# RWKV stage of a hybrid trunk: a strictly ordered opening with fill products in it, two directions filled before their evictions, 44 products kept for the end

## The chip, the cores and the metric

The kernel runs on one core of a Trainium2 chip. The metric is the device time of one execution in microseconds. All arithmetic is in fp32 (the large projections in a high and a low fp32r part).

## What is computed

One inference step of a trunk of two layers with 128 context tokens and 1024 latent tokens of width 1024. In each layer the normed and modulated input is projected to four branches (mLSTM, RG-LRU, retention, RWKV-7), each in both directions of time; their outputs, times a SiLU gate, go together through one output projection to the residual. The change is in the RWKV branch:

```python
def rwkv_scan(r, w, k, v, kk, bb, s0):
    def step(s, xs):
        rt, wt, kt, vt, kkt, bt = xs
        sa = jnp.einsum('bhij,bhj->bhi', s, -kkt)
        s = s * wt[:, :, None, :] + sa[..., None] * bt[:, :, None, :] + vt[..., None] * kt[:, :, None, :]
        return s, jnp.einsum('bhij,bhj->bhi', s, rt)

def rwkv_branch(u, mu, w0, w2, a0, a2, k_k, k_a, r_k, s0, rows):
    ...
    for d in range(N_DIR):
        w_log = -jax.nn.softplus(-(w0[d] + lw @ w2[d])) - 0.5
        decay = jnp.exp(-jnp.exp(w_log))
        a = jax.nn.sigmoid(a0[d] + la @ a2[d])
        kt = k * (1.0 + (a - 1.0) * k_a)
        seqs = (r, decay, kt, v, kk, kk * a)
        ...
        y, sf = rwkv_scan(*seqs, s0[:, d])
    bonus = jnp.sum(r * k * r_k, -1, keepdims=True) * v
    y = (head_norm(outs[0] + outs[1]) + bonus) * jax.nn.silu(g)

# of the layer
u = h @ p['w_in']
y = jnp.concatenate([y_a, y_b, y_c, y_d], -1) @ p['w_out']
x = x + gate * y
```

## The kernel before

A layer has three parts: the input projection, with the mLSTM, RG-LRU and retention branches laid over it; the RWKV stage (`rw_all`, from L160); and `tail` (L1171), which multiplies the last part of the output projection, adds the residual and norms for the next layer.

**Units.** The RWKV stage works the sequence in chunks of 64. Nine units follow one another: two halves of the chunks for each of four pairs of heads, and one unit for the context tokens at index 6. Forward and backward direction ("f", "b") of a unit run side by side. The steps of a unit are: the block of its pair (`rw_block`: token shift, norm, sums over heads); `early` (`rw_prep`: the lora products `a<-lora_x`, decay scans, the operands AR and BK); `scores` (products `a<-AR,BK`, masked into SC); `solve` (L494: the inverse of 32x32 triangular blocks; the blocks go by DMA from SC through DRAM into the tiles iU and iN, iN is cleared by two memsets on GpSimd, 62 operations on VectorE, DMAs back into SC); `tokens` (transposes); `mid` (L526: five steps of products that put the blocks together, evicted into NT, Wt, SC, AR, UV); and the chain (`rw_chain`, L577: sixteen gaps in which state ST and UV follow from each other in tiles `u`, then the output `u` evicted into y). `rw_final` norms y and stores it.

**Fills.** Between these steps TensorE gets "fill" products, L1289, `main<-yt,ow`, and modulation products, `main<-wmod`, from one generator: the input projection of the RWKV pairs 1 to 3 (96 products each), in layer 0 also the next layer's modulation, and the output projection of what is finished. `pull(x)` takes x of them, `drain(q)` takes all up to a mark. The output projection loads an old value through the tile xi, adds to it and stores it, and once four units' worth is finished it covers the RWKV pairs 0 to 2 too. Their weights (`ow`, 6 buffers) and inputs (`yt`, 16 buffers) come by DMA; all DMAs are issued from one queue, SP.

**Order.** A scheduler orders instructions on each engine by a priority (`level` 0 to 3, 3 first) and by what it reckons to be ready. While `self.strict` is true, each product that goes through `pm`, `ptr` or `fill` is chained to the one before, so TensorE follows the program. The opening of the stage (all up to `mid` of unit 0, with the preparation of unit 1) is not strict and runs at level 1; the units are strict. In a unit `pull(rate)` is called in each gap, with rate = what is left / units left / 20. PSUM tiles: `a` (two buffers), `v` and `u` (two banks each, one buffer), `main`.

Of the kernel before, what the change touches and what calls it, by code (L numbers as in the profile page):

```python
# [16 lines left out]
MUL, ADD, SUB, MAX, MIN = ALU.mult, ALU.add, ALU.subtract, ALU.max, ALU.min  # L17
# [13 lines left out]
class B:  # L31
# [130 lines left out]
    def rw_all(self, l):  # L162
# [5 lines left out]
        N = len(units)  # L168
# [3 lines left out]

        def block(n):
            p = units[n][0]
            if n < N and p not in P:
                for q in LATE:
                    if p is None or q == p:
                        self.drain(q)
                with self.level(1):
                    P[p] = self.rw_block(l, p)  # L180

        def early(n):
            p, su = units[n]
            S[n] = {}
            for dn in "fb":
                with self.level(1):
                    S[n][dn] = self.rw_prep(P[p], dn, 0 if p is None else 8 * su if dn == "f" else 8 - 8 * su, self.rd[n % 2])
                yield

        def operands(n, lv):  # L190
            with self.level(lv):
                for dn in "fb":
                    self.rw_operands(P[units[n][0]], dn, S[n][dn])
# [32 lines left out]

        run = lambda g: [None for _ in g]
        self.strict = False
        block(0)
        run(early(0))  # L230
        operands(0, 1)
        run(scores(0, 1))
        solve(0)
        run(tokens(0))
        run(early(1))
        operands(1, 1)
        run(scores(1, 1))
        self.drain(1)
        run(mid(0))
        self.last, self.strict = None, True  # L240
        total = self.nfill
        left = lambda: total - self.pulled
        finish = None
        for n, (p, su) in enumerate(units):
            if n + 1 < N:
                solve(n + 1)
            rate = left() / (N - n) / (16 + (4 if n + 1 < N else 0))
            steps = self.rw_chain(l, P[p], su, S[n], S[n - 1] if su else None)
            tok = tokens(n + 1) if n + 1 < N else iter(())
            pre = iter(())  # L250
            for gap in range(16):
# [17 lines left out]
                if gap in (12, 14):  # L269
                    next(pre, None)  # L270
            run(tok)
            run(pre)
            with self.level(3):
# [5 lines left out]
            for k in range(5):  # L279
                next(m, None)  # L280
                self.pull(rate * 0.8)
                if k >= 2:
                    next(sc, None)
            run(m)
            run(sc)
            if su or p is None:
                finish = P[p]
        with self.level(1):
            self.rw_final(l, finish)
# [11 lines left out]
    def drain(self, what):  # L301
        while what not in self.done:
            next(self.fills)

# [189 lines left out]
    def rw_solve(self, S):  # L494
# [15 lines left out]
        self.a.copy(U[b], N[b][:, ::-1])  # L510
        self.g.memset(N, 0.0)
        self.g.memset(N[:, ::33], -1.0)  # L512
        Uv, Nv = U.rearrange("p (r k) -> p r k", k=32), N.rearrange("p (r k) -> p r k", k=32)
# [12 lines left out]
    def rw_mid(self, S):  # L526
# [30 lines left out]
        for d, dn in enumerate("fb"):  # L557
            AR, SC, UV = (S[dn][n] for n in ("AR", "SC", "UV"))
            for g in range(4):
                for h in range(2):  # L560
                    for q in range(2):
                        self.pm(ps[HV[h], q, d, g], UV[HV[q], 2 * g + q, HV[h]], SC[HV[q], 4 * q + g, h, 0:64])
            self.a.copy(AR[:, 0::2, 0], ps[:, 0, d])
            self.v.tensor_copy(AR[:, 1::2, 0], ps[:, 1, d])
        yield
        ps = self.pst2("u").rearrange("p d (g h x) -> p d g h x", h=2, x=64)
        for d, dn in enumerate("fb"):
            SC, UV = S[dn]["SC"], S[dn]["UV"]
            for g in range(4):
                for h in range(2):  # L570
                    for q in range(2):
                        self.pm(ps[HV[q], d, g, h], SC[HV[q], 4 * q + g, h, 0:64], SC[HV[q], 4 - 4 * q + g, h, 0:64])
            uv = lambda q: UV[HV[q], q::2].rearrange("p g (h i) -> p g h i", h=2)
            self.a.copy(uv(0), ps[HV[0], d])
            self.v.tensor_copy(uv(1), ps[HV[1], d])

    def rw_chain(self, l, X, su, S, prev):  # L577
# [13 lines left out]
        for i in range(8):  # L591
# [21 lines left out]
            yield  # L613
        po = self.pst2("u")
        for di, dn in enumerate("fb"):
            s = S[dn]
            if p is None:
                for q in range(4):
                    self.dma(self.o["rwkv_s"][l, di, q], s["ST"][:, 4 + q])
            ps = po[:, di].rearrange("p (c i) -> p c i", i=64)  # L620

            first = True
            for j, a, _ in D[dn]:
                if a is not None:
                    for h in HV:
                        self.pm(ps[h, j], a[h], s["AR"][h, j, 1], start=first, stop=False)
                    first = False
            for i, (j, a, _) in enumerate(D[dn]):
                for h in range(2):
                    self.pm(ps[HV[h], j], s["UV"][:, j, HV[h]], s["SC"][:, 4 * (j % 2) + j // 2, h, 64:128], start=False, stop=(i == 7))  # L630
            y = X["y"][:, 64 * s["c0"]:64 * s["c0"] + 512].rearrange("p (c i) -> p c i", i=64)
            if su or (p is None and di):
                self.tt(self.v, y, ps, y, ADD)
            else:
                self.a.copy(y, ps)

# [808 lines left out]
MLB = 1  # L1445
YOB = 16
HV = (slice(0, 64), slice(64, 128))

# [154 lines left out]
```

## Time and profile before

| | us |
|---|---|
| median of three runs | 4093.64 |
| lowest, highest | 4092.91, 4098.87 |
| the profiled execution | 4099.86 |
| its span, first to last instruction | 4098.1 |
| TensorE busy in the span | 3655.4 (89%) |
| VectorE, ScalarE, GpSimd busy | 2001.2, 1295.3, 1135.2 |

The mean granted clock of TensorE was 0.923 of its full speed. The RWKV stage lies, by the first and last of its products, between about 1102 and 2059 us in the first layer and between 3151 and 4051 us in the second; the rest of the span is input projection, tail and start. In what follows "opening" is from the first lora product to the first chain product, "body" the units 0 to 7, "end" from the last unit's last chain product to the tail's first product. TensorE appears in the trace with two records for one fp32 product. A wait in square brackets is the idle time of the engine just before the row, with what ended it.

### The profile page before, as it was taken

The page shows a single profiled execution, that of the slowest core. Times are in us where ns is not written, and L with a number is a line of the kernel's source. Part 1 is how long each engine was busy: PE and PEld are TensorE (multiplying, and loading weights), DVE is VectorE, ACT ScalarE, POOL GpSimd, SP SyncE. Part 2 cuts the span into 40 slices and gives each one's busy share as a digit, 9 for nine tenths or more (in the row PEclk, how much of TensorE's full clock was granted, in tenths as well). Part 3 has the DMA queues.
Part 4 walks back from the last instruction along what each step waited for, and adds up shares of the span by engine and source line. Part 5 has one row for each costly group of instructions (what it writes and reads, how often), then busy time and mean ns, then how long its engine had stood idle before and what let it go on. Part 6 is the DMA issues. An engine that isn't in the chain of part 4 may idle for free. (4 is left out here: it accounts for less than half of the span.)

```text
span 4098.1 us, 69587 instructions
## 1 busy us (share of the span) xinstructions
PE 3655.4 (89%) x28050; PEld 2844.9 (69%) x28050; DVE 2001.2 (49%) x3917; ACT 1295.3 (32%) x2102; POOL 1135.2 (28%) x1052
## 2 busy tenths in 40 slices
PE   6899999999959898989779999999998598988896
PEld 3889899999544455555468898999985455555554
DVE  4454643333264565565274545533331746656544
ACT  3244422122223333332152535122122234333312
POOL 4223234533221112212043232434431212212200
PEclk8999999999969999999989999999998699989998
DMA  5434443443624543444644434543445144433445
GB/s 210 120 120 138 122 133 121 121 132 123 214 62 146 158 137 119 120 122 116 191 157 132 122 115 129 139 127 94 136 137 180 29 130 131 131 113 101 117 141 166
DMA packets 413550, 538.02 MB, mean 131 GB/s; under 512 B 141708, under 2 KB 322700, under 8 KB 413228
## 3 DMA queue, kind: packets, MB, share of 16 engines
q1 hardware_dynamic: 413228, 533.57, 42.8%
q8 instruction: 221, 3.62, 0.4%
q14 instruction: 101, 0.83, 0.1%
HBM read 387.17 MB, written 146.25 MB: 130 GB/s over the span
## 5 line engine op out<-in xcount | busy, mean ns | idle before, releaser
L1289 PE MATMUL main<-yt,ow 128*128 128x384 f32 x2592 | 963.9, 512 | 18.0 <-DVE xi L48 12.0
L1289 PEld LDWEIGHTS main<-yt,ow 128*128 128x128 f32 x2592 | 473.9, 194 | 314.2 <-issue 37.2
L59 PE MATMUL main<-hh,wring_h 128*128 128x384 f32 x1824 | 648.5, 356 | 26.8 <-DVE st L1283 15.5
L59 PE MATMUL main<-hl,wring_h 128*128 128x384 f32 x1824 | 645.4, 354 | 13.7 <-DVE hl L44 10.9
L59 PE MATMUL main<-hh,wring_l 128*128 128x384 f32 x1824 | 641.4, 352 | 0.0
L44 POOL TENSOR_TENSOR wring_l<-raw,wring_h 128x1024 fp32r<-128x1024 f32 x100 | 243.8, 2442 | 592.2 <-ACT wring_h L1240 444.5
L59 PEld LDWEIGHTS main<-hh,wring_h 128*128 128x128 f32 x1824 | 359.7, 197 | 40.1 <-DVE st L1283 16.2
L59 PEld LDWEIGHTS main<-hl,wring_h 128*128 128x128 f32 x1824 | 359.6, 197 | 25.6 <-DVE hl L44 13.5
L59 PEld LDWEIGHTS main<-hh,wring_l 128*128 128x128 f32 x1824 | 359.6, 197 | 7.6 <-issue 1.3
L59 PE MATMUL main<-wring_h,hh 128*128 128x256 f32 x864 | 261.3, 302 | 14.0 <-DVE st L1283 13.0
L59 PE MATMUL main<-wring_l,hh 128*128 128x256 f32 x864 | 257.2, 298 | 0.0
L59 PE MATMUL main<-wring_h,hl 128*128 128x256 f32 x864 | 256.5, 297 | 0.0
L44 DVE TENSOR_TENSOR tm<-iU,iN 64x31 f32<-64x31 f32 (+15 forms) x558 | 191.9, 344 | 92.8 <-POOL iN L512 77.9
L44 POOL TENSOR_TENSOR t<-s_k,bb 128x512 f32<-128x512 f32 x36 | 60.4, 1678 | 576.3 <-ACT bb L56 576.3
L1283 DVE COPY st<-main 128x384 f32<-128x384 f32 (+1 forms) x168 | 86.1, 512 | 258.1 <-PE main L59 227.0
L44 DVE TENSOR_TENSOR iN<-iN,tm 64x31 f32<-64x31 f32 (+15 forms) x558 | 198.0, 355 | 16.5
L59 PEld LDWEIGHTS main<-wring_h,hh 128*128 128x128 f32 x864 | 173.9, 201 | 19.6 <-DVE st L1283 14.0
L59 PE MATMUL a<-AR,BK 64*128 64x128 f32 x1152 | 125.4, 324 | 58.3 <-POOL BK L44 30.4
L59 PEld LDWEIGHTS main<-wring_h,hl 128*128 128x128 f32 x864 | 173.9, 201 | 4.6 <-issue 0.4
L59 PEld LDWEIGHTS main<-wring_l,hh 128*128 128x128 f32 x864 | 173.6, 201 | 3.0
L59 PEld LDWEIGHTS a<-AR,BK 64*128 64x128 f32 x1152 | 108.4, 222 | 96.1 <-POOL BK L44 34.9
L1240 ACT CAST wring_h<-raw 128x1024 fp32r<-128x1024 f32 x100 | 103.4, 1046 | 219.8 <-PE main L59 169.4
(332 smaller groups left out, 6110.4 us busy)
## 6 DMA issues: line engine op xcount, KB each, us to landing
raw<-in_w_in SPq DMA_DIRECT2D x100, 512.0 KB
ow<-in_w_in SPq DMA_DIRECT2D x144, 256.0 KB
ow<-in_w_out SPq DMA_DIRECT2D x144, 256.0 KB
yt<-h SPq DMA_DIRECT2D x144, 192.0 KB
mrb<-mlrow SPq DMA_DIRECT2D x48, 384.0 KB
x<-xi SPq DMA_DIRECT2D x96, 192.0 KB
yt<-y SPq DMA_DIRECT2D x90, 192.0 KB
wmod<-in_w_mod SPq DMA_DIRECT2D x64, 256.0 KB
```

The costliest lines, as they stand in the source:

```text
L44: return e.tensor_tensor(out=out, in0=a, in1=b, op=op)
L59: return self.t.matmul(out, l, r, start=start, stop=stop)
L1240: self.a.copy(hi, raw)
L1283: self.v.tensor_copy(q[:, :w], ps[:, :w])
L1289: return self.pe(self.t.matmul(*a, **k))
```

## The change

First, the opening is strict too, at levels 2 and 3 for unit 0, and after each of its steps fill products are taken (`weave(g, x)`: x after each step of g). Second, the rate in the units leaves 44 products (`RESERVE`), which are taken at the end: 11 ahead of `rw_final` of the last unit, 33 behind it; this `rw_final` has level 3 instead of 1. Third, in the last two steps of `mid` and in the chain's output both directions' products come first and all evictions behind them. Fourth, the two memsets of the solve move from GpSimd to VectorE. The number of instructions of each kind stays as it is.

```diff
-        def block(n):
+        def block(n, lv=1):
...
-                with self.level(1):
+                with self.level(lv):
                     P[p] = self.rw_block(l, p)
...
-        def early(n):
+        def early(n, lv=1):
...
-        run = lambda g: [None for _ in g]
-        self.strict = False
-        block(0)
-        run(early(0))
-        operands(0, 1)
-        run(scores(0, 1))
+        def weave(g, x):
+            for _ in g:
+                self.pull(x)
+
+        self.last, self.strict = None, True
+        block(0, 2)
+        weave(early(0, 3), 8)
+        operands(0, 3)
+        weave(scores(0, 3), 3)
         solve(0)
-        run(tokens(0))
-        run(early(1))
+        weave(tokens(0), 3)
+        weave(early(1, 1), 4)
         operands(1, 1)
-        run(scores(1, 1))
+        weave(scores(1, 1), 4)
         self.drain(1)
-        run(mid(0))
-        self.last, self.strict = None, True
+        weave(mid(0), 2)
...
-            rate = left() / (N - n) / (16 + (4 if n + 1 < N else 0))
+            rate = (left() - RESERVE) / (N - n) / (16 + (4 if n + 1 < N else 0))
...
-        with self.level(1):
+        self.pull(RESERVE / 4)
+        with self.level(3):
             self.rw_final(l, finish)
         self.finished += 1
         self.drain("all")
...
-        self.g.memset(N, 0.0)
-        self.g.memset(N[:, ::33], -1.0)
+        v.memset(N, 0.0)
+        v.memset(N[:, ::33], -1.0)
...
         for d, dn in enumerate("fb"):
-            AR, SC, UV = (S[dn][n] for n in ("AR", "SC", "UV"))
+            SC, UV = S[dn]["SC"], S[dn]["UV"]
...
+        for d, dn in enumerate("fb"):
+            AR = S[dn]["AR"]
             self.a.copy(AR[:, 0::2, 0], ps[:, 0, d])
             self.v.tensor_copy(AR[:, 1::2, 0], ps[:, 1, d])
...
+        for d, dn in enumerate("fb"):
+            UV = S[dn]["UV"]
             uv = lambda q: UV[HV[q], q::2].rearrange("p g (h i) -> p g h i", h=2)
             self.a.copy(uv(0), ps[HV[0], d])
             self.v.tensor_copy(uv(1), ps[HV[1], d])
...
-            y = X["y"][:, 64 * s["c0"]:64 * s["c0"] + 512].rearrange("p (c i) -> p c i", i=64)
+        for di, dn in enumerate("fb"):
+            y = X["y"][:, 64 * S[dn]["c0"]:64 * S[dn]["c0"] + 512].rearrange("p (c i) -> p c i", i=64)
             if su or (p is None and di):
-                self.tt(self.v, y, ps, y, ADD)
+                self.tt(self.v, y, po[:, di], y, ADD)
             else:
-                self.a.copy(y, ps)
+                self.a.copy(y, po[:, di])
...
+RESERVE = 44
```

**TensorE, second layer, from the end of retention into the opening.** `ntr` are the transposes of retention's norm, `sq` and `rk` feed sums over heads. Before:

```order
L1289 MATMUL main<-yt,ow 128x384 x20
L682 MATMUL ntr<-ident,rty 128x128 x4
L1289 MATMUL main<-yt,ow 128x384 x11
L682 MATMUL ntr<-ident,rty 128x128 x4
L1289 MATMUL main<-yt,ow 128x384 x9
L682 MATMUL ntr<-ident,rty 128x128
L1289 MATMUL main<-yt,ow 128x384 x8
L59 MATMUL a<-lora_x,lora_w 128x512 x2
L59 MATMUL v<-sq,bones 128x512
L1289 MATMUL main<-yt,ow 128x384
L59 MATMUL a<-lora_x,lora_w 128x512 x2
```

And now:

```order
L689 MATMUL ntr<-ident,rty 128x128 x9
L59 MATMUL a<-lora_x,lora_w 128x512 x2
L59 MATMUL v<-sq,bones 128x512
L1296 MATMUL main<-yt,ow 128x384 x8
L59 MATMUL a<-lora_x,lora_w 128x512 x2
L59 MATMUL v<-sq,bones 128x512
L1296 MATMUL main<-yt,ow 128x384 x8
L59 MATMUL v<-rk,bones 128x512 x2
L59 MATMUL a<-AR,BK 128x128 x8
L1296 MATMUL main<-yt,ow 128x384 x3
L59 MATMUL a<-AR,BK 128x128 x8
```

The fill products moved from between retention's last steps to between the opening's.

**VectorE, first layer, inside the first solve.** `tm` and `iN` are the solve's operations, the others the preparation of unit 1 and the masks of its scores. Before:

```order
L44 TENSOR_TENSOR tm<-iU,iN 64x207
L52 TENSOR_SCALAR tw<-tw 128x512
L44 TENSOR_TENSOR iN<-iN,tm 64x23x9
L400 SCALAR_TENSOR_TENSOR bb<-scan_87,tw 128x512
L44 TENSOR_TENSOR tm<-iU,iN 64x220
L44 TENSOR_TENSOR iN<-iN,tm 64x22x10
L52 TENSOR_SCALAR tw<-tw 128x512
L44 TENSOR_TENSOR tm<-iU,iN 64x231
L44 TENSOR_TENSOR AR<-kk,tw 128x8x63
```

And now:

```order
L44 TENSOR_TENSOR tm<-iU,iN 64x207
L44 TENSOR_TENSOR iN<-iN,tm 64x23x9
L44 TENSOR_TENSOR tm<-iU,iN 64x220
L44 TENSOR_TENSOR iN<-iN,tm 64x22x10
L44 TENSOR_TENSOR tm<-iU,iN 64x231
L44 TENSOR_TENSOR iN<-iN,tm 64x21x11
L44 TENSOR_TENSOR tm<-iU,iN 64x240
L44 TENSOR_TENSOR iN<-iN,tm 64x20x12
```

The other work stands behind 46 of the 62 operations instead of behind 17.

**TensorE, second layer, behind the last unit's chain.** `yq` feeds the head sums of `rw_final`, `t_yh` and `t_hi` are the tail's operands. Before:

```order
L59 MATMUL u<-AR,ST 64x64 x16
L59 MATMUL u<-SC,UV 64x64 x16
L59 MATMUL v<-yq,bones 128x512 x2
L59 MATMUL main<-t_yh_33021,t_hi 128x384 x4
L59 MATMUL main<-t_yl_33022,t_hi 128x384
```

And now:

```order
L59 MATMUL u<-AR,ST 64x64 x16
L59 MATMUL u<-SC,UV 64x64 x16
L1296 MATMUL main<-yt,ow 128x384 x5
L59 MATMUL v<-yq,bones 128x512
L1296 MATMUL main<-yt,ow 128x384 x6
L59 MATMUL v<-yq,bones 128x512
L1296 MATMUL main<-yt,ow 128x384 x33
L59 MATMUL main<-t_yh_33021,t_hi 128x384
```

All 44 kept products stand ahead of the tail here; in the first layer the last 18 stand among the tail's products, in groups of three.

## Rows read from the trace of the kernel before

**Rows 1.** Stretches: length; busy of PE, PEld, DVE, ACT, POOL; PEclk, DMA share, GB/s.

```profile
1101.90:1223.70 121.80, 79.19 (x665) 54.55 (x664) 72.02 (x151) 38.59 (x68) 40.31 (x29) 0.71 0.31 93
1223.70:1966.10 742.40, 663.56 (x7061) 397.24 (x7061) 415.01 (x986) 246.24 (x452) 141.60 (x116) 0.95 0.44 129
1966.10:2033.10 67.00, 58.96 (x383) 32.13 (x382) 23.12 (x63) 0.63 (x1) 0.00 (x0) 0.97 0.61 180
2033.10:2059.30 26.20, 3.20 (x4) 0.80 (x4) 6.55 (x8) 9.16 (x10) 7.13 (x3) 0.59 0.91 315
...
3150.80:3265.40 114.60, 59.92 (x585) 45.08 (x584) 72.38 (x151) 36.18 (x63) 40.40 (x29) 0.59 0.18 51
3265.40:3969.50 704.10, 625.19 (x6952) 392.91 (x6952) 414.42 (x984) 242.77 (x446) 141.73 (x116) 0.95 0.41 120
3969.50:4033.80 64.30, 54.83 (x371) 30.04 (x370) 21.43 (x58) 0.63 (x1) 0.00 (x0) 0.98 0.62 184
4033.80:4051.30 17.50, 4.15 (x4) 1.00 (x4) 4.39 (x7) 6.14 (x7) 0.00 (x0) 0.50 0.87 293
```

**Rows 2.** Timeline of PE, second layer, end of retention: start, length, instruction, count.

```profile
3118.74 13.12 PE L1289 MATMUL main<-yt,ow 128*128 128x384 f32 x40
...
3132.13 7.26 PE L1289 MATMUL main<-yt,ow 128*128 128x384 f32 x22
...
3150.84 1.13 PE L59 MATMUL a<-lora_x,lora_w 64*128 64x512 f32 x4
```

**Rows 3.** Timeline of POOL, first and second layer, end of retention.

```profile
1044.76 0.45 POOL L44 TENSOR_TENSOR rtR<-rtR,rtU 64x128 f32<-64x128 f32 x1
...
3074.58 0.45 POOL L44 TENSOR_TENSOR rtR<-rtR,rtU 64x128 f32<-64x128 f32 x1
3125.12 3.19 POOL L44 TENSOR_TENSOR rty<-rty,nss 128x1152 f32<-128x1152 f32 x1 [50.10 <-ACT nss L56]
```

**Rows 4.** Timeline of PE, second layer, opening; idle before a row in brackets.

```profile
3241.15 0.59 PE L59 MATMUL v<-ident,SC 32*32 32x32 f32 x4 [12.96 <-DMA SC<-dN]
```

**Rows 5.** Timeline of DVE, first layer: the first solve's first and last operation.

```profile
1150.96 0.20 DVE L44 TENSOR_TENSOR tm<-iU,iN 64x31 f32<-64x31 f32 x1 [7.64 <-POOL iN L512]
...
1195.43 0.18 DVE L44 TENSOR_TENSOR iN<-iN,tm 64x31 f32<-64x31 f32 x1
```

**Rows 6.** Page, part 5: one of the solve's two operations: busy, mean ns, idle.

```profile
L44 DVE TENSOR_TENSOR tm<-iU,iN 64x31 f32<-64x31 f32 (+15 forms) x558 | 191.9, 344 | 92.8 <-POOL iN L512 77.9
```

**Rows 7.** Waits of PE in both bodies, layer by layer: us in total, times, longest.

```profile
PE u L59 <- DVE y L44: 18.6, 3, 6.5
...
PE v L59 <- DVE AR L564: 8.3, 8, 1.1
PE u L59 <- DVE UV L575: 8.1, 8, 3.5
PE u L59 <- ACT y L635: 6.1, 5, 1.9
...
PE main L1289 <- DMA wmod<-in_w_mod: 1.0, 3, 0.6
...
PE u L59 <- DVE y L44: 20.3, 3, 7.0
...
PE u L59 <- ACT y L635: 8.4, 5, 2.6
PE v L59 <- DVE AR L564: 7.5, 7, 1.1
```

**Rows 8.** SP and PE timelines in one unit: the solve's way back, first use.

```profile
1464.31 4.44 SPq L81 DMA_DIRECT2D SC<-dN  x8
...
1486.49 0.75 PE L59 MATMUL v<-ident,SC 32*32 32x32 f32 x64
```

**Rows 9.** Timelines of PE and SP at the end of the second layer's stage.

```profile
4051.35 1.65 PE L59 MATMUL main<-t_yh,t_hi 128*128 128x384 f32 x4 [11.22 <-ACT t_yh L1202]
...
4030.31 13.16 SPq L81 DMA_DIRECT2D xs<-x  x24
```

More of the change, by code (lines that the diff above doesn't have):

```diff
@@ L185, in early @@
             for dn in "fb":
-                with self.level(1):
+                with self.level(lv):
                     S[n][dn] = self.rw_prep(P[p], dn, 0 if p is None else 8 * su if dn == "f" else 8 - 8 * su, self.rd[n % 2])
@@ L270, in rw_all @@
                     next(pre, None)
-            run(tok)
-            run(pre)
+            weave(tok, 0)
+            weave(pre, 0)
             with self.level(3):
@@ L283, in rw_all @@
                     next(sc, None)
-            run(m)
-            run(sc)
+            weave(m, 0)
+            weave(sc, 0)
             if su or p is None:
                 finish = P[p]
-        with self.level(1):
+        self.pull(RESERVE / 4)
+        with self.level(3):
             self.rw_final(l, finish)
@@ L302, in drain @@
         while what not in self.done:
-            next(self.fills)
+            next(self.fills, None)
     def rw_block(self, l, p):
@@ L613, in rw_chain @@
             yield
-        po = self.pst2("u")
+        po = self.pst2("u").rearrange("p d (c i) -> p d c i", i=64)
         for di, dn in enumerate("fb"):
-            s = S[dn]
+            s, ps = S[dn], po[:, di]
             if p is None:
@@ L619, in rw_chain @@
                     self.dma(self.o["rwkv_s"][l, di, q], s["ST"][:, 4 + q])
-            ps = po[:, di].rearrange("p (c i) -> p c i", i=64)
             first = True
```

## The prediction

> **What bounds the kernel now.** I read the table of stretches first. In the bodies of the two RWKV stages TensorE is busy 663.56 of 742.4 us and 625.19 of 704.1 us [rows 1], so there time falls only if TensorE gets less to do or waits less. The reader should see next how different the openings are: 79.19 of 121.8 us busy at a granted clock of 0.71, and 59.92 of 114.6 us at 0.59 [rows 1]. They run a chain of small steps and waits, and the fill products that could cover them have been used up: in program order 56 output products and 16 modulation products (layer 0), 95 (layer 1) stand before the first lora product. The timeline of the end of retention shows those products in wide blocks, 40 records of them 13.12 us long between a retention product and the norm's transposes [rows 2]. A product is two records. A block of 22 took 7.26 us, so the 18 more of the other cost 13.12 - 7.26 = 5.86 us, 0.65 us a product [rows 2]. The waits of the bodies come third: they are led by waits of one direction's products for the other direction's eviction [rows 7]. Last, the ends of the stages: 26.2 and 17.5 us with TensorE busy 3.20 and 4.15 us, but DMA at 0.91 and 0.87 of its share, 315 and 293 GB/s [rows 1].
>
> The sum is made against the profiled execution's own 4099.86 us (span 4098.1). The median of the three runs is 4093.64, so 6 us come off at the end.
>
> **The opening.** The fills leave the end of retention, which then runs on its own latencies. GpSimd's retention recurrence ends at 1044.8 (layer 0) and 3074.6 (layer 1) [rows 3], 57 and 76 us ahead of the first lora product. What remains is some ten score and state products with a mask each, and then a norm: in layer 1 it took from 3118.74, where the last retention product was done, to 3128.31 [rows 2, 3], 9.6 us; transposes and their evictions follow. I allow 28 us from the end of the recurrence: first lora product at 1073 and 3103, where they were at 1101.9 and 3150.84 [rows 1, 2].
>
> From there TensorE has more work than before. Its own part: the layer 1 opening, with only one fill product in it, was busy 59.92 us at clock 0.59 [rows 1]; at full clock that is 59.92 x 0.59 = 35 us. Fill in program order: 96 output products and 25 modulation products in layer 0, 105 output products in layer 1. At 0.65 us, and 0.87 for a modulation product (an estimate: 512 columns instead of 384), this is 62 + 22 = 84 us and 68 us. To this I add 5 us of waits and 4 us of low clock at the start, since TensorE idles at the end of retention: 1073 + 35 + 84 + 9 = 1201 and 3103 + 35 + 68 + 9 = 3215 for the first chain product, against 1223.7 and 3265.4. That is **-23 and -50**.
>
> The other path to the same point is the latency path, and it must be shorter for this to hold. Before, the first solve took from 1150.96 to 1195.6 [rows 5], because operations of the second unit's preparation were put between its own 62; these are some 0.35 us each [rows 6], 22 us, and with gaps about 26. In the new order 46 of them stand in a row, so the matrices are back some 18 us earlier, and the 12.96 us wait for them [rows 4] goes. The whole path from lora to chain was 121.8 and 114.6 us [rows 1]; less 18 and less the 13, it is some 90. It lies below the 112 to 128 of TensorE, so TensorE sets the end, if the DMAs of the solve are not held up; that is a rival below.
>
> In strict order a fill product that waits for its weights holds every product behind it. The bodies have run so all along, and there the wait for weights was 1.0 us in all, in 3 times [rows 7]; I take zero, and for the upper bound the loss of the whole gain, 73 us. The Trainium skill, TensorE: Matmul & The Clock Gate, section Part 3: Packing small matmuls, says that matmuls are strictly first in, first out and are never reordered. By that rule nothing passes a fill that waits, the row does not contradict it, and the sum would lie between the -73 taken here and 0 for this term.
>
> **Fewer fills in the bodies.** Units 0 to 7 hold 447 output and 39 modulation products instead of 485 and 47 in layer 0, and 444 instead of 490 in layer 1. At the same prices: 38 x 0.65 + 8 x 0.87 = **-32**, 46 x 0.65 = **-30**. This is on the path, because TensorE is busy nine tenths there [rows 1]. Unit 8 has 61 instead of 68 and 55 instead of 61: -4.5 and -4, and with the y wait between its directions **-7 and -6**.
>
> **Both directions first, then the evictions.** The waits for y fall away: 18.6 and 6.1 us in layer 0, 20.3 and 8.4 in layer 1 [rows 7]. The evictions that ended late (up to 7.0 us, DVE being in the middle of a solve) are next needed when the same banks are filled again, four steps of the next unit's middle later. The waits of the middle for AR and UV, 8.3 and 8.1 us, of which 3.5 is in the opening, and 7.5 in layer 1 [rows 7], go only in half: the next step now finds two pairs of evictions outstanding instead of one, with two fill products over them. So 24.7 + 6.4 = **-31**, 28.7 + 3.8 = **-32**.
>
> **The end.** 44 products, 28.6 us at 0.65, now stand behind the last unit. Before the tail's first product TensorE waited 11.22 us [rows 9], which covers as much; that leaves 17 in layer 1, where 33 of the 44 stand before the tail. In layer 0, 18 stand among the tail's own products, so less: 5 at the least. By DMA it is more. Unit 8 moved 180 GB/s over 67 us for 68 products [rows 1], 0.18 MB for each, so 44 bring 7.8 MB to a stretch that was already at 293 to 315 GB/s: 25 to 27 us. I take **+16 and +22**, nearer to the DMA rows in layer 1, since that stretch was full.
>
> **The memsets on DVE.** No row shows one there. The solve's operations of at most 256 elements take 0.18 to 0.4 us [rows 5, 6]; 1024 elements should be 0.2 to 1.4 us, nine times a layer. DVE gets 1 us later to what is queued behind, and waited for GpSimd's memset 77.9 us in all [rows 6], which may shrink. Bounds -10 to +15 a layer; taken **+5 each**, mostly for evictions behind a solve.
>
> **Sum:** -23 -50 -32 -30 -7 -6 -31 -32 +16 +22 +5 +5 = -163. 4099.9 - 163 = 3937, less 6 for the median: **3931**, told as 3930.
>
> **Rivals.**
> (a) The opening's gain is not had. In the new order the solve's small DMAs stand on SP's queue between loads of weights whose buffers come free only when fill products have run; TensorE, in strict order, then waits in the middle for the inverse, as it did for 12.96 us [rows 4]. Against it: 25 output products in layer 1 stand between the last score and the middle as cover. If all is lost: 3930 + 73 = 4003; I put it at **3995**.
> (b) The end jams. If the 44 products run at unit 8's rate, 67 us / 68 = 0.985 us [rows 1], they take 43 us, less 11 covered: 32; and if the tail's loads also stand behind the 13.16 us of residual loads on SP [rows 9], some 45 a layer instead of 19: 3930 + 52 = **3982**.
> (c) The fused evictions only move the wait: the refill of the same banks waits for y instead. Then the 63 us stay: **3993**. Against it are the four steps between.
> (d) The clock gains too: bodies at 0.95 [rows 1] go to 1.0 once fewer waits break them. 5% of 1289 busy us is 64; about three quarters of it: **3880**.
> (e) Slower: the solve becomes the bound of every unit. Its matrices were on the way at 1464.31 to 1468.75 and first used at 1486.49 [rows 8], 17.7 us of slack. Units become some 7 us shorter and the memset takes 1, so about 10 are left. If DVE's new order (a solve with its evictions behind two directions) delays it by more than those 10, each further us costs 16 of them (eight solves in each layer that a body waits for). From 20.2 us of delay on all of the 163 is lost; at 21.2 the time is **4110**. Nothing in the trace delays DVE that much, as it is busy 415 of 742 us [rows 1].
> (f) The change moves nothing that counts, its gains and losses cancelling: 4094.
>
> **How the numbers follow.** Forecast 0.53, with its own range 3900 to 3960 from the bounds of the end and the memsets; (a) 0.14, (b) 0.12, (c) 0.08, (d) 0.07, (e) 0.03, (f) 0.03. The range reaches from (d) to (a): 3870 to 4005; beyond it lie (e), (f) and tails. A measurement of this kernel can tell 0.2%, 8 us, from no change: faster 0.94, same 0.03, slower 0.03.
>
> **What would show it.** Right: in the profile after, the first lora product near 1073 and 3031 (3103 less the 72 us of layer 0), no fill between retention products, and fills at full clock between lora and the first chain product; no wait for y in the bodies' list, and AR and UV waits halved; ends of 40 us with DMA still near 0.9. Wrong: a wait for SC<-dN of over 10 us at the first middle (a), or in later units (e); ends of over 60 us (b); a new wait of u for y in the middle (c).

## The result, and the profile after

The changed kernel takes 3981.7 us (median of 4 runs, 3971.49 to 3988.03) against 4096.26 us (4 runs of the kernel before): a ratio of 0.9715, 95% interval 0.9689 to 0.9742. The profiled execution took 3979.25 us with a span of 3977.5 us, where before it was 4098.1. So about 115 to 121 us are gone; the prediction had summed 163 (3930 us). Its range, 3870 to 4005, holds the time. Sign and places were right, the size was not: by the medians 52 us of the forecast gain are missing (by the profiled executions 42), and part of what did come came from another place.

The table of stretches of the kernel after, with the columns of [rows 1]. In order: from the end of GpSimd's retention recurrence to the first lora product, opening, body, last unit, end, and in the first layer the tail up to the next projection's first product:

```profile
1052.80:1086.10 33.30, 21.33 (x89) 19.11 (x89) 6.33 (x8) 6.74 (x9) 3.19 (x2) 0.50 0.18 61
1086.10:1228.30 142.20, 128.44 (x844) 65.19 (x843) 85.70 (x184) 44.61 (x79) 36.16 (x25) 0.96 0.56 171
1228.30:1903.50 675.20, 624.48 (x6959) 375.57 (x6959) 415.70 (x969) 242.11 (x450) 133.93 (x102) 0.95 0.45 132
1903.50:1956.90 53.40, 52.02 (x371) 29.75 (x371) 16.11 (x51) 0.00 (x0) 0.00 (x0) 1.00 0.57 165
1956.90:1991.40 34.50, 24.14 (x59) 12.43 (x57) 11.52 (x19) 9.65 (x11) 7.20 (x3) 0.80 0.91 302
1991.40:2032.10 40.70, 36.77 (x141) 26.67 (x141) 26.37 (x65) 18.54 (x39) 5.34 (x9) 0.96 0.76 249
3040.70:3074.10 33.40, 21.40 (x90) 19.15 (x90) 6.33 (x8) 6.74 (x9) 3.22 (x2) 0.50 0.20 71
3074.10:3208.20 134.10, 115.34 (x797) 67.06 (x796) 81.18 (x170) 42.75 (x76) 34.34 (x25) 0.91 0.46 138
3208.20:3834.90 626.70, 580.74 (x6855) 366.06 (x6855) 414.31 (x975) 239.70 (x444) 133.63 (x102) 0.96 0.43 126
3834.90:3885.50 50.60, 48.36 (x359) 27.40 (x359) 15.98 (x50) 0.00 (x0) 0.00 (x0) 1.00 0.57 170
3885.50:3933.40 47.90, 35.74 (x91) 18.06 (x92) 14.33 (x24) 7.25 (x9) 0.00 (x0) 0.89 0.81 254
```

Against [rows 1] the reader sees three things. The openings are full now (128.44 of 142.2 us busy at a clock of 0.96, where it was 79.19 of 121.8 at 0.71), but longer. The bodies are 67 and 77 us shorter. And the stretch ahead of the opening runs at a granted clock of 0.50, the lower level (1.2 GHz); with the fills among it, the same stretch before was 56.7 and 75.8 us long, at 1.00 and 0.97:

```profile
1045.20:1101.90 56.70, 56.70 (x234) 33.75 (x232) 6.95 (x11) 10.65 (x17) 3.20 (x2) 1.00 0.69 230
3075.00:3150.80 75.80, 75.80 (x290) 48.03 (x288) 6.62 (x9) 11.89 (x20) 3.22 (x2) 0.97 0.60 189
```

Where the time went, by the same marks in both profiled executions (first layer / second layer, us):

| stretch | before | after | difference | forecast |
|---|---|---|---|---|
| all ahead of the end of retention's recurrence | 1045.2 / 992.5 | 1052.8 / 1008.7 | +7.6 / +16.2 | 0 / 0 |
| end of retention | 56.7 / 75.8 | 33.3 / 33.3 | -23.4 / -42.5 | -29 / -48 |
| opening | 121.9 / 114.6 | 142.2 / 134.1 | +20.3 / +19.5 | +6 / -3 |
| body, units 0 to 7 | 742.3 / 704.0 | 675.2 / 626.7 | -67.1 / -77.3 | -58 / -57 |
| last unit | 67.0 / 64.3 | 53.4 / 50.6 | -13.6 / -13.7 | -7 / -6 |
| end and tail | 49.5 / 64.4 | 75.2 / 92.0 | +25.7 / +27.6 | +16 / +22 |
| sum | | | -50.5 / -70.2 | -72 / -91 |

(The forecast column is the prediction's terms sorted into these stretches and rounded, the memset's +5 within the body.)

The waits of TensorE in the body of the kernel after answer to [rows 7]: some lines of the first layer, then of the second (us in total, times, longest).

```profile
PE v L59 <- ACT NT L544: 15.6, 3, 6.2
PE u L59 <- DVE UV L44: 7.7, 5, 5.0
...
PE u L59 <- DVE UV L582: 1.4, 1, 1.4
```

```profile
PE v L59 <- ACT NT L544: 9.5, 3, 4.9
PE v L59 <- DMA SC<-dN: 8.0, 5, 3.4
...
PE v L59 <- DVE AR L569: 0.3, 1, 0.3
```

No wait for y is left, and those of the middle for AR and UV (L569, L582) are almost gone. In their place stands one for NT, ScalarE's copy in the middle's first step, 15.6 and 9.5 us; before it had 1.8 and 1.1. In the second layer there is also a wait for the solve's way back. Three lines of the same lists before, two of the first layer and one of the second:

```profile
PE a L59 <- DVE SC L44: 12.7, 6, 4.0
...
PE v L59 <- ACT NT L541: 1.8, 2, 1.1
```

```profile
PE v L59 <- ACT NT L541: 1.1, 1, 1.1
```

Theories and rivals that this profile leaves. Of the opening: its small gain is all there is, since TensorE has more to do there and begins at low clock; or the gain is had, and another part eats it. Of the bodies: the wait for y has moved to NT, through ScalarE's queue, and gave less than its length; or NT's wait is another matter, and y gave what was forecast. Of the products kept for the end: they cost at the end what they give in the units; or there is a better number of them.

### The profile page after: what moved, and what is told of

The parts are those of the page before. It is cut to its first block, busy times and chain, and to the rows that moved or that the text cites. A ratio compares the mean times of both kernels' runs of the same rounds, so it can differ in the third digit from the quotient of the medians.

```text
span 3977.5 us, 69524 instructions
## 1 busy us (share of the span) xinstructions
PE 3648.6 (92%) x28050; PEld 2831.0 (71%) x28050; DVE 2033.8 (51%) x3953; ACT 1291.7 (32%) x2102; POOL 1110.7 (28%) x1016
## 5 line engine op out<-in xcount | busy, mean ns | idle before, releaser
L1296 PE MATMUL main<-yt,ow 128*128 128x384 f32 x2592 | 989.0, 520 | 25.1 <-DVE xi L48 17.5
L59 PE MATMUL main<-hl,wring_h 128*128 128x384 f32 x1824 | 647.8, 355 | 21.7 <-DVE hl L44 19.6
L59 PE MATMUL main<-wring_h,hh 128*128 128x256 f32 x864 | 265.0, 307 | 17.7 <-DVE st L1290 17.1
L44 DVE TENSOR_TENSOR tm<-iU,iN 64x31 f32<-64x31 f32 (+15 forms) x558 | 202.2, 362 | 15.9
L1288 ACT COPY st<-main 128x384 f32<-128x384 f32 (+1 forms) x168 | 73.4, 437 | 270.2 <-PE main L59 264.3
```

Of the source, the lines that this page charges most:

```text
L44: return e.tensor_tensor(out=out, in0=a, in1=b, op=op)
L59: return self.t.matmul(out, l, r, start=start, stop=stop)
L1288: self.a.copy(q[:, :w], ps[:, :w])
L1296: return self.pe(self.t.matmul(*a, **k))
```

## Experiments: one part at a time

Each of these four kernels is the kernel before with one part of the change.

The opening alone (strict, levels 2 and 3, fills between its steps):

```diff
+        self.last, self.strict = None, True
+        block(0, 2)
+        weave(early(0, 3), 8)
...
+        weave(mid(0), 2)
```

> The kernel before with the opening alone changed (strict order, levels, fill products woven in). Theory (the ledger of intervals of the changed kernel): retention's end 23 and 42 us shorter, the opening 20 us longer in each layer, 8 modulation products (7 us) and some 7 output products (5 us) fewer in the units: 38 us less than before, 0.991. Rival, as I had predicted: 73 us less in the two openings and 12 in the units, 0.979. Rival 2: the strict opening, with the solve's transfers behind weight loads, is worth nothing by itself: 1.000 +- 0.002.

Measured: 4076.5 us, ratio 0.9947 (0.9924 to 0.9970), so -21 us. By stretches the end of retention and the opening together gave -0.5 and -21.7 us (33.3 + 144.8 against 56.7 + 121.9; 33.3 + 135.4 against 75.8 + 114.6), in the kernel after -3.1 and -23. No other part had eaten the gain; it was not there.

The three fused evictions alone:

```diff
+        for d, dn in enumerate("fb"):
+            AR = S[dn]["AR"]
...
+        for d, dn in enumerate("fb"):
+            UV = S[dn]["UV"]
...
+        for di, dn in enumerate("fb"):
+            y = X["y"][:, 64 * S[dn]["c0"]:64 * S[dn]["c0"] + 512].rearrange("p (c i) -> p c i", i=64)
```

> The kernel before with only the evictions behind both directions. Theory: the waits for y go (25 and 29 us), those for AR and UV in half: 63 us less, 0.985. Rival (the ledger of the changed kernel, where units and last unit became 28 us shorter than their fewer products account for, layer by layer): 80 us or more less, 0.980. Rival 2: the wait only moves to the refill of the same banks, and the kernel gains less than 20 us, 0.995 or above.

Measured: 4014.8 us, ratio 0.9795 (0.9759 to 0.9831), so -83 us, more than two thirds of the whole change. The bodies shrank by 48.0 and 39.4 us, the last unit by 1.4 and 0.1.

The products kept for the end alone, with the last norm's level 3:

```diff
-            rate = left() / (N - n) / (16 + (4 if n + 1 < N else 0))
+            rate = (left() - RESERVE) / (N - n) / (16 + (4 if n + 1 < N else 0))
...
-        with self.level(1):
+        self.pull(RESERVE / 4)
+        with self.level(3):
             self.rw_final(l, finish)
```

> The kernel before with only the 44 products kept for the end (and the last norm at level 3). Theory: units 0 to 7 lose 39 products each layer (25 us), the last unit 5 and some of its waits for old values (5 to 14 us), the end gets 26 and 30 us longer: 10 us less in each layer, 0.995. Rival: the end costs as much as the units gain, 1.000 +- 0.002. Rival 2: the tail's loads stand behind the products' loads and the first products of the next projection come late: slower, 1.004.

Measured: 4083.49 us, ratio 0.9969 (0.9949 to 0.9989), -14 us. Bodies -20.8 and -29.3, last unit -12.0 and -11.8, end and tail +21.2 and +27.1: of 74 us that the units gave, the ends took 48 back, and the stretches ahead of retention's end were 9 and 7 us longer.

The memsets on VectorE alone:

```diff
-        self.g.memset(N, 0.0)
-        self.g.memset(N[:, ::33], -1.0)
+        v.memset(N, 0.0)
+        v.memset(N[:, ::33], -1.0)
```

> The kernel before with only the two memsets of the solve on VectorE. Theory: 1 us of VectorE for each of 18 solves, mostly beside other work: 1.000 to 1.002. Rival: VectorE no longer waits behind GpSimd's queue (77.9 us of such waits in the trace of before), evictions come earlier: 0.995 or below. In both the input projections are as before; if the first recurrence of retention ends 8 us later or more here too, that shift in the changed kernel is no matter of the edits.

Measured: 4104.62 us, ratio 1.0006 (0.9985 to 1.0026): no difference. On VectorE the large memset (64x1024) took 0.912 us and the small one 0.085; on GpSimd they had taken 0.944 and 0.148.

The four singles add up to -21 - 83 - 14 + 0 = -118 us (the memset's +7 is within its interval), and the whole change measured -115. The intervals of the four together leave some 20 us (an estimate from their widths), so that a larger loss or gain of the parts on each other is ruled out and a smaller one is not; one of about 15 us is told under what stays open. The other side of the opening, the kernel after with the opening of before, closes the sum:

```diff
-        self.last, self.strict = None, True
-        block(0, 2)
-        weave(early(0, 3), 8)
...
+        self.strict = False
+        block(0)
+        run(early(0))
```

> The changed kernel with the opening of before (not strict, level 1, fills early). Theory: the opening is worth here what it is alone, 21 us (ledger 37 less the noise of the input projection): 0.977. Rival: with units 90 us faster the fills that the opening leaves to them weigh more, or the solve's slack is gone, and it is worth 35 us or more: 0.980. Rival 2: nothing, 0.9715.

Measured: 4002.51 us, ratio 0.9758 (0.9713 to 0.9804). Between it and the kernel after lie 0.0043 of 4096, 18 us, beside the 21 of the opening alone; the intervals of these two overlap, so that this difference by itself proves little. By stretches the end of retention and the opening of the kernel after were 5.1 and 20.5 us shorter than here.

## Experiments: which eviction it was

Only the chain's output fused, the products of both directions into y first and then the evictions:

```diff
+        po = self.pst2("u").rearrange("p d (c i) -> p d c i", i=64)
...
+        for di, dn in enumerate("fb"):
+            y = X["y"][:, 64 * S[dn]["c0"]:64 * S[dn]["c0"] + 512].rearrange("p (c i) -> p c i", i=64)
```

> The kernel before, with only the chain's output written for both directions before its evictions. Theory: the two waits for y (24.7 and 28.7 us in the bodies, 2 us in each last unit) and the slower products right behind them (some 10 us in all) make most of the 84 us that the whole fusing gave: 60 to 65 us less, 0.985. Rival: a wait for another eviction takes half of it back, 30 us, 0.993, and the middle steps are worth more than I gave them.

Only the two steps of the middle:

```diff
+        for d, dn in enumerate("fb"):
+            AR = S[dn]["AR"]
...
+        for d, dn in enumerate("fb"):
+            UV = S[dn]["UV"]
```

> The kernel before, with only the two steps of the middle (AR and UV) written for both directions before their evictions. Theory: what is left of the 84 us: 20 to 25 us less, 0.994 (my prediction had 6.4 and 3.8 us in the bodies). Rival: nothing, since the next step waits for two pairs of evictions: 0.999.

Measured: y alone 4075.64 us, ratio 0.9950 (0.9928 to 0.9972); the middle alone 4060.56 us, ratio 0.9908 (0.9874 to 0.9941). In the bodies y gave -18.4 and -10.9 us, the middle -30.0 and -27.7; together that is -48.4 and -38.6, and the fusion of all three had given -48.0 and -39.4. The medians agree less well: 20 and 36 us, 56 together, where all three gave 83. The profiled execution of the middle alone, 4044.2 us, lay 16 us below its median, so that its share in the bodies is the less certain one. The prediction had it the other way round: 24.7 and 28.7 for y, 6.4 and 3.8 for the middle.

Why y gave less is seen in the waits of TensorE in the first layer's body, y alone fused:

```profile
PE v L59 <- ACT NT L541: 14.6, 3, 6.4
PE a L59 <- DVE SC L44: 12.9, 6, 4.0
```

The 24.7 us for y [rows 7] are gone, and NT has 14.6. SC, the scores of the next unit, has the 12.7 of before still (12.9). The same place in the program, one of the three long ones, on TensorE, ScalarE and VectorE in turn (start, length, instruction, idle before it):

```profile
1557.04 1.15 PE L59 MATMUL u<-AR,ST 64*64 64x64 f32 x32
1558.12 1.15 PE L59 MATMUL u<-SC,UV 128*64 128x64 f32 x32
1559.20 0.75 PE L59 MATMUL v<-ident,SC 32*32 32x32 f32 x64
1559.88 1.56 PE L1289 MATMUL main<-yt,ow 128*128 128x384 f32 x4
1567.89 1.08 PE L59 MATMUL v<-NT,SC 32*32 32x32 f32 x64 [6.45 <-ACT NT L541]
```

```profile
1563.62 0.63 ACT L56 ACTIVATE yq<-y 128x512 f32<-128x512 f32 x1 [5.16 <-DVE y L44]
1566.30 1.28 ACT L56 ACTIVATE s_r<-u_r,rwc_omu 128x128 f32<-128x128 f32 x4 [2.05 <-POOL AR L44]
1567.49 0.35 ACT L541 COPY NT<-v 128x256 f32<-128x256 f32 x1
```

```profile
1559.03 2.78 DVE L48 SCALAR_TENSOR_TENSOR BK<-ta,t 128x256 f32<-128x256 f32 x2
1561.73 1.26 DVE L44 TENSOR_TENSOR AR<-kk,tw 128x504 f32<-128x504 f32 x2
1562.91 1.27 DVE L44 TENSOR_TENSOR y<-u,y 128x512 f32<-128x512 f32 x2
```

TensorE goes through both directions without a stop now, and then stands for 6.45 us before the products with NT. The products for NT were done at 1559.95, and its copy takes 0.35 us, but on ScalarE it is queued behind yq (the square of y for the norm), which waits 5.16 us for VectorE's y, and behind s_r, which waits 2.05 us for GpSimd. VectorE's y itself stands behind 4 us of BK and AR. So the late y still holds TensorE, by way of ScalarE's queue.

The middle alone, at the same place, keeps the wait for y and shows what such a wait costs beside its own length:

```profile
1549.41 1.15 PE L59 MATMUL u<-AR,ST 64*64 64x64 f32 x32
1550.48 1.15 PE L59 MATMUL u<-SC,UV 128*64 128x64 f32 x32
1557.57 1.98 PE L59 MATMUL u<-AR,ST 64*64 64x64 f32 x32 [5.93 <-DVE y L44]
1559.47 1.97 PE L59 MATMUL u<-SC,UV 128*64 128x64 f32 x32
```

The same two groups of products take 1.15 us each ahead of the wait and 1.98 and 1.97 behind it: the granted clock was 1.00 for the first two and 0.50 for the last two, having fallen while TensorE stood. So a wait can cost more than its length. The middle gave more than its waits too: in its first layer's body the idle time fell from 78.8 to 58.2 us, and the busy time from 663.6 to 654.1 with the same products. That the clock made this second part is argued from the rows above, not shown by a run of its own. Of the idle time, the middle's waits for AR (8.3) and UV (6.1 without the one at the first chain product) are gone from the body, and the wait for SC went from 12.7 to 6.1 (in the second layer from 10.2 to 3.4).

The test of the queue: the kernel after, with ScalarE's squares of y and its token shift ordered behind the middle's copies. `chain` only sets the order on the engine and adds no wait.

```diff
-        self.a.copy(Wt, ps)
+        self.hold = self.a.copy(Wt, ps)
...
-            self.act(z[:, h], y[:, h], ACT.Square)
+            self.chain(self.hold, self.act(z[:, h], y[:, h], ACT.Square))
...
-        self.act(s, u, ACT.Identity, scale=omu)
+        self.chain(self.hold, self.act(s, u, ACT.Identity, scale=omu))
```

> The changed kernel, in which ScalarE's copies NT and Wt of a unit's middle come ahead of the squares yq of the finished pair and of the shift of the next block (an order on ScalarE alone). In the changed kernel TensorE waits for NT 15.6 and 9.5 us in the bodies, 3 times each, with those two kinds of instruction ahead of NT on ScalarE, waiting for VectorE's y and GpSimd's AR. Theory: this is where the wait for y went when the evictions were put behind both directions; without them ahead it goes: 15 to 25 us less than the changed kernel, 0.966 of before. Rival: the next step then waits as long for VectorE (AR, SC), whose queue is what is late: no change, 0.9715.

Measured: 3956.87 us, ratio 0.9649 (0.9603 to 0.9695). The point lies 25 to 27 us below the kernel after; the intervals overlap slightly (0.9695 and 0.9689). In the trace the mechanism is plain. From the list of TensorE's waits in the first body, led by UV, and in the second:

```profile
PE u L60 <- DVE UV L45: 10.8, 8, 3.9
...
PE v L60 <- DVE AR L570: 3.9, 2, 3.5
```

```profile
PE v L60 <- DMA SC<-dN: 7.8, 5, 3.2
...
PE v L60 <- DVE AR L570: 5.8, 3, 4.0
```

The wait for NT is gone from both. The first layer's body is 14.2 us shorter than in the kernel after, the second's only 2.9: there AR took back 5.5 of the 9.5 us and SC<-dN stayed. So NT's 25 us were worth some 17 in the bodies. The run moves both kinds of instruction, the squares and the shift, and does not tell which of the two held NT longer.

## Experiments: the opening and the end

Fourteen fill products pulled ahead of the strict opening, into the end of retention, to see whether they cost less there than in the opening:

```diff
+        self.pull(14)
         self.last, self.strict = None, True
```

> The changed kernel with 14 fill products taken before the strict opening begins, so that they stand between retention's last steps (12 of them in one block where GpSimd's recurrence is waited for). Theory: retention's end, 33.3 us at a granted clock of 0.50, has 12 us of waits that cover 9 us of products and a clock that these keep up; it gets at most 3 us longer, and the openings lose 9 to 12 us: 10 to 20 us in all below the changed kernel, 0.967 of before. Rival: products push retention's chain back by all of their time, 9 us, as the fills of before did: no change, 0.9715.

Measured: 3967.86 us, ratio 0.9689 (0.9662 to 0.9716), 11 to 14 us below the kernel after, with intervals that overlap. The end of retention kept its length (32.1 and 35.2 us) and its clock rose from 0.50 to 0.83 and 0.74 in the two layers; the opening became 134.4 and 126.9 us, 7.8 and 7.2 shorter.

The same with the order on ScalarE, and then with 28 products:

```diff
+        self.pull(14)
...
+        self.hold = self.a.copy(Wt, ps)
```

> The same with the 14 early fill products of the run before. Theory: both gains, 13 and 15 to 25 us: 0.963. Rival: 0.969, as with the 14 products alone.

```diff
+        self.pull(28)
...
+        self.hold = self.a.copy(Wt, ps)
```

> The same with 28 early products. Theory: in layer 0 retention's end has waits and a clock of 0.50 to cover them, in layer 1 they stand ahead of its score products (12, 10 and 6), where only the first 12 are covered: retention's end 0 to 5 us longer in layer 0 and 8 to 10 in layer 1, openings 18 us shorter each: 0.961. Rival: no better than 14, 0.963 or more.

Measured: 3940.38 us, ratio 0.9621 (0.9563 to 0.9680) with 14, and 3979.44 us, ratio 0.9710 (0.9660 to 0.9761) with 28. The first is the fastest kernel of the study and beats both kernels, the one after too: its interval ends below that one's 0.9689. With 28 the end of retention grows to 39.8 and 45.6 us, while the opening shortens by 2 us at most (126.8 and 123.4 against 128.7 and 124.0). So 14 products fit into the stretch almost for nothing, and of the further 14 the most part only moved the start of the opening; no number between was run. That explains a part alone: of the 56 us between the two profiled executions (39 between the medians), retention's end and opening account for 4.5 and 9.5 us, the bodies for 4.4 and 14.0, the stretches ahead of retention's end for 11.0 and 14.9. Why these were longer too was not found.

Twenty products kept for the end instead of 44, in the kernel after:

```diff
-RESERVE = 44
+RESERVE = 20
```

> The changed kernel with 20 products kept instead of 44. Theory: the gain of the 44 (13 us by themselves) is the units' 25 us and the last unit's 12 us a layer less an end of 15 to 29 us more; with 20, units keep 12 us more each, the last unit 3 to 6, the ends get 10 to 14 us shorter: about the same as 44, within 8 us, 0.970 to 0.973. Rival: the last unit's rate was all of it and is lost: 0.975 or more. Rival 2: the ends grow faster than the count, DMA being full, and 20 is better by 10 to 20 us: 0.968.

Measured: 3978.33 us, ratio 0.9717 (0.9683 to 0.9751), the same as with 44. End and tail are 57.7 and 76.2 us instead of 75.2 and 92.0, but the bodies 680.1 and 650.4 instead of 675.2 and 626.7 and the last unit 7.2 and 6.1 longer. What the ends save, 33 us, the units pay, 42; the stretch ahead of the second stage was 12.8 us shorter.

## Why the prediction was right or wrong

**The opening, -23 and -50: the mechanism was right, the size was not.** It came out at -3 and -23. The first lora product came at 1086.10, where it was to be at 1073: 7.6 us because all ahead of it was later, and 5 because the bare end of retention took 33.3 us instead of 28. In the second layer it came at 3074.07, where 3031 was named, most of it because the first layer had not given its share. The timeline of TensorE, kernel after, second layer, from the end of retention on:

```profile
3055.49 0.64 PE L59 MATMUL rN<-rtR,rtQX 128*128 128x64 f32 x2
3055.92 0.63 PE L59 MATMUL rN<-rtV,rsd 128*128 128x64 f32 x2
...
3069.86 1.11 PE L689 MATMUL ntr<-ident,rty 128*128 128x128 f32 x4 [9.47 <-POOL rty L44]
...
3074.07 2.52 PE L59 MATMUL a<-lora_x,lora_w 64*128 64x512 f32 x4
...
3150.41 0.49 PE L59 MATMUL a<-AR,BK 64*128 64x128 f32 x2 [3.75 <-POOL BK L44]
3151.96 2.07 PE L59 MATMUL a<-AR,BK 64*128 64x128 f32 x14 [1.06 <-ACT ta L56]
3153.96 5.02 PE L1296 MATMUL main<-yt,ow 128*128 128x384 f32 x8
...
3160.00 2.85 PE L1296 MATMUL main<-yt,ow 128*128 128x384 f32 x8
...
3185.61 0.75 PE L59 MATMUL v<-ident,SC 32*32 32x32 f32 x64
...
3191.37 0.75 PE L59 MATMUL v<-NT,SC 32*32 32x32 f32 x64 [3.51 <-ACT NT L544]
```

The forecast that no fill stands between the retention products came true, and with it they run slowly: pairs start 0.43 us apart. In the kernel before, the same kind among the fills, they started 0.22 apart:

```profile
3083.34 0.39 PE L59 MATMUL rN<-rtR,rtQX 128*128 128x64 f32 x2
3083.56 0.39 PE L59 MATMUL rN<-rtV,rsd 128*128 128x64 f32 x2
```

Then the transposes wait 9.47 us for the norm, as the prediction had read off [rows 3]. In the opening, the prediction's sum was 35 (own products) + 68 (fills) + 9 (waits and low clock) = 112 us; by these records it was 39 + 76 + 19 = 134 (in the first layer 38 + 90 + 14 = 142, for 35 + 84 + 9 = 128). So the term that failed most is that of the waits and the low clock, 9 us for what was 19 of waits alone in the second layer. The own part had been scaled by the clock, 59.92 x 0.59, and the fills priced at 0.65 us, as if all of it ran at full speed in the new order; but behind a wait it does not (a group of 8 fill records took 5.02 us here behind two waits, at a granted clock of 0.55, and 2.85 the next time, at 1.00). The waits are nine, of 0.31 to 3.75 us, eight of them on the chain of the opening's own steps (such as BK, ta, NT). Fills stand between these steps, but unevenly: 25 products in a row ahead of the middle, where nothing was waited for but xi, and 4 or none at the waits for BK and ta. No run spread them otherwise.

**Rival (a)**, that the solve's matrices come back too late, fell: `v<-ident,SC` at 3185.61 has no wait, where it had 12.96 us [rows 4]. The first solve took 35.0 and 35.6 us in the two layers, not the 26 that the prediction had for it, but its last transfer was issued 33 and 21 us ahead of that product. The wait for weights in the openings is nil as well. The Trainium skill (TensorE: Matmul & The Clock Gate, section Part 3: Packing small matmuls) says that matmuls keep strictly to first in, first out; the trace agrees, the fills stand in it in program order, but nothing was lost by it, and the price by the rule's upper bound, the whole gain, did not arise.

**Fewer fills and both directions first, -63 and -62 together: right in sum, for the wrong reasons.** With the memset's +5 the bodies were to lose 58 and 57; they lost 67.1 and 77.3. Of this the fusion had been given 31 and 32 and made 48 and 39. By the records of the two bodies, TensorE's idle time fell by 28 and 33 us, the time of the fills by 26 and 27, and the units' own products, the same in number, took 13 and 17 us less: a term that the prediction did not have. Two steps failed. "The waits for y fall away" was true of the waits, not of the time: rival (c) in part, the wait moved, though not to the refill of the same banks, as it had been put, but to NT through ScalarE's queue. The prediction asked only who needs y's banks next, not what stands behind y on the other engines. And "AR and UV go only in half" was far too low: they went wholly, and half or more of the wait for SC with them. In the second layer the prediction had counted AR's 7.5 us alone; UV had 9.6 us there too, 3.5 of them in the opening. That y gave less than forecast and the middle more brought the sum near; this part was luck.

**The last unit, -7 and -6**, was -13.6 and -13.7. One step that failed is the price: 0.65 us for a product, though the unit itself had run at 0.985 us for one, the very number that rival (b) used. Even at that pace 7 products are 6.9 us, half of what went. The other is idle time, which fell from 8.0 to 1.4 us in the first layer, and for it the prediction had only the wait for y, of 0.8 us there. It was waiting for the old values that the output products add to (TensorE, kernel before, first layer):

```profile
PE main L1289 <- DVE xi L48: 5.3, 5, 2.5
```

With 44 products kept, alone or in the kernel after, this wait is gone from the stretch; with 20 kept 4.1 us of it are left. So fewer fills there save waits for loads, not only products.

**The end, +16 and +22**, was +26 and +28. The estimate by DMA was nearer than that by TensorE; in the first layer the prediction took the smaller one, since 18 products stand among the tail's own, and lost 10 us: the tail grew from 23.3 to 40.7 us. The end of the second layer in the kernel after, on TensorE:

```profile
3901.91 6.09 PE L1296 MATMUL main<-yt,ow 128*128 128x384 f32 x12 [5.47 <-DVE xi L48]
...
3931.68 2.20 PE L1296 MATMUL main<-yt,ow 128*128 128x384 f32 x6 [0.91 <-DVE xi L48]
```

Each group waits for xi again, eight times, 0.46 to 5.47 us; 33 products took from 3894.3 to 3933.4, 1.18 us each. Rival (b) had taken 0.985 us, so that the pace was worse still; but its other half, the tail's loads late by 13 us more, did not come: from the tail's first product to the end of the span it is 44.1 us, where it was 46.8. Some 27 us a layer were lost, not its 45: (b) fell as it was put.

**The memsets, +5 each,** cost nothing that can be measured.

**The other rivals.** (d), a gain of clock, did not come as it was put: the bodies have 0.95 and 0.96, where both had 0.95. (e), the solve as the bound, is there in small: SC<-dN, which had no line in the second body's list before, has 8.0 us in 5 waits there. The 17.7 us of slack of [rows 8] were those of one unit; by the same measure, from the last transfer's issue to the first use, the second layer's units from the third on had 7.9 to 28.2 us before and have -0.7 to 21.5 now, two of them with nothing left. That is far from the loss of the whole gain. (f) fell by the interval.

**What stays open.** The stretch ahead of the second RWKV stage was 16 us longer, where the forecast had nothing. Its counterpart in the first layer scatters between 1045 and 1061 us among kernels that have the same code there (1052.7 with the memsets alone, 1045.3 with the middle alone), so the +7.6 says nothing. In the second layer the kernels with both the new opening and 44 kept products have 1007 to 1022, all others 990 to 1000, with 20 kept products 995.9. There the kernel after has waits that stand nowhere among the larger ones of before:

```profile
PE main L59 <- DVE hl L44: 9.6, 4, 5.6
PE mup L59 <- DMA mV<-ut_ml_vo: 6.2, 1, 6.2
```

In this size both stand in all five kernels that have the new opening and 44 kept products (8.5 to 10.8 and 6.0 to 7.2 us), and in none of the four that have one of the two without the other: the opening alone, the 44 alone, the kernel after with the old opening, and with 20 kept products. So this loss belongs to the two parts together, but what in them makes the transfer of mV and hl late was not found. Between the two profiled executions TensorE's idle time in that stretch rose by 10.9 us in all and its busy time by 5.3.

By the table, what the forecast is short of the profiled execution's -121 (42 us) is this: the openings and the end of retention 47, the stretches ahead 24, the ends 15; against it the bodies gave 29 more and the last units 14 more.

## What to carry to other kernels

When a wait is taken away, look at what stands behind the late instruction on each engine's queue, not only at who needs its buffer: here VectorE's y went on holding TensorE by way of ScalarE's copies, until those were put first. Price a product at the pace of the stretch in which it stands (0.65, 0.985 and 1.18 us here for one and the same), since a fill that is moved into or out of a stretch paced by loads moves the loads too. And a stretch that is stripped of its fills does not run at its own latencies alone: it runs at the clock that is then granted (0.50 here).

## What the runs showed of the hardware that was not expected

- The bare end of retention ran at a granted clock of 0.50 for all of its 33 us, with TensorE busy 21 of them, and its pairs of small products 0.43 us apart; in the kernel before, where these stretches had fills among them and a clock of 1.00 and 0.97, they were 0.22 apart. With 14 fills ahead of the opening the stretch had 0.83 and 0.74, and its length was 32.1 and 35.2 us.
- Behind a wait of 5.93 us, in which the granted clock fell from 1.00 to 0.50, the same 32 products took 1.98 us that took 1.15 ahead of it. Such a wait costs more than its length.
- A memset of 64x1024 fp32 took 0.912 us on VectorE and 0.944 on GpSimd: which of the two does it made no difference to the time.
